# One-core recurrent trunk: small transfers on GpSimd's queue, and first slabs with two contraction tiles of four output tiles

## The chip, the cores and the metric

The kernel runs on one core of one Trainium2 chip. The metric is the device time of one execution in microseconds, lower is better, and the time of a kernel is the median of its runs.

## What is computed

One inference step of a two-layer decoder trunk (width 2048) for 288 tokens: one prompt of 256 and eight samples of 4 tokens that share the weights. Cut to what matters here:

```
layer 0:  u = x @ w_in_e                       # 2048 -> q, k, v, lru_x, z, lru_gate (6144) and 16 gate columns
          q, k, v, lru_x = causal_conv(width 4, with the last 3 rows of state_conv)
          a  = gated_delta_rule(q, k, v, g, beta, state_delta)  # 8 heads, S is 128 x 128 for each head and sample
          b  = rg_lru(lru_x, r, i, state_lru)
          mix = concat(a, b) @ w_out_e
layer 1:  u = x @ w_in_o ; mix = mlstm(q, k, v, i, f, state_c, state_n, state_m) @ w_out_o   # 8 heads
each:     x = LN(alpha*x + mix) ; x = LN(alpha*x + sqReLU-MLP(x)) ; x = x + sigmoid(x Wg) * (p Wp)
outputs:  y, and the new conv, delta, lru and mLSTM states of prompt and samples
```

All values are f32. The 16 gate columns of layer 0 give g (the decay, as a running sum along the tokens) and beta of the eight delta heads.

## The kernel before

**Matrix products.** The tokens lie along the free dimension (288 columns). An f32 product is made of three passes in a rounded format: `ah`, `bh` are the rounded values ("hi") of the activations and `al`, `bl` the rests ("lo"), `hi` and `lo` the same of the weights, and a contraction tile costs the passes hi·ah, lo·ah and hi·al, all into one PSUM tile `acc` (L416). Weights come as slabs of eight 128x128 blocks (512 KB): SyncE (SP) issues the transfer into one of four `raw` buffers (L394), ScalarE casts it to `hi` (L294), VectorE subtracts to get `lo` (L295), and TensorE spends 24 matmuls on it. `Trunk.convert` issues one slab, `top_up` keeps up to three slabs converted ahead in the mixers. An output tile (16 contraction tiles, 48 matmuls) is two slabs. There are 20,064 such matmuls, and they take the bulk of the time.

**The start.** `Trunk.load` issues on SP, in this order: x tiles 0 and 1, the first slab in two halves, x tiles 2 and 3, x tiles 4 to 7, two slabs, x tiles 8 to 15, parameters and constants. A slab holds eight contraction tiles of one output tile. The first four output tiles (`z`, `v`, `k`, `q` of head 0) are taken in groups: the lower eight contraction tiles of all four, then the upper eight, so that the fourth slab can run with x tiles 0 to 7. After three of these slabs (`GATES_AT = (3, 1)`) `gate_products` makes the 16 gate columns from a 256 KB slab `w_ab`: 32 matmuls with 32 columns of weights each, once with `ah` and once with `al`; VectorE and ScalarE then make g and beta in rows of 8 partitions, called `bl` in the trace (`delta_gates`, L701 to L727), which end with a scan (L715).

**The side work.** While TensorE runs through slabs, `tick` lets generators go one step every 12 matmuls: the eight delta heads (`delta_head`), the sample part (`delta_sample`), the eight RG-LRU blocks, and in layer 1 the mLSTM heads. Their small matmuls stand between the slabs' matmuls in TensorE's order, which is fixed when the program is built. An engine works its instructions off in order, so a small matmul whose input is late holds the slabs behind it.

**Small transfers.** SP's queue also carries, between the slabs: the convolution's state into `cin` and out of it (`sconv`, `conv`, 28 KB), `gcb` (a head's row of g from the scratch `dgc` in DRAM, broadcast to 128 partitions, 144 KB), the sample states `S` in and out (256 KB, 32 loads and 16 stores, `delta_sample`, L1010 and L1074), `wri`, `delta_p`, and in layer 1 `ngb`, `cn` in and out (514 KB) and `mc_p`. ScalarE's queue carries the gates' small transfers: `dgc`, then `dds` (g, beta, last g to DRAM) and `rs` (the same back, along the partitions); in layer 1 `dng`, `mds`, `mrs`, `dw`, `w`, `dsc`, `scB`. Pool (GpSimd) issues no transfer; it copies small pieces, for instance `ks` and `zs` (a head's sample columns, L861, L862), `gcs` (from `gcb`, L863), `v` and `k` of an mLSTM head (L1317).

**Head 0.** `dgc` and `rs` wait for the scan. From `gcb` comes the decay mask `dm`, from `rs` the factors `sw`; VectorE then makes `mq`, `X`, and the 32x32 transposes `t` (L791), and TensorE starts head 0's inversion with a small matmul that takes `t` and `cm`.

Of the kernel before, what the change touches and what calls it, by code (L numbers as in the profile page):

```python
# [37 lines left out]
C_FOLD = C_LAST + 128  # L38
C_D32 = C_FOLD + 32
# [6 lines left out]
def const_table():  # L46
# [16 lines left out]
    c[:, C_FOLD:C_FOLD + 32] = j % 32 == np.arange(32)[None]  # L63
# [79 lines left out]
def lay_out(a):  # L143
    d = {}
# [14 lines left out]
    d["w_in_e"] = pack_w(a["w_in_e"][0][:, :6144])  # L159
    d["w_ab"] = pack_gates(a["w_in_e"][0][:, 6144:])  # L160
# [46 lines left out]
GATES_AT = (3, 1)  # L207
LATE = 12

# [9 lines left out]
class Trunk:  # L219
# [73 lines left out]
    def split(self, hi, lo, src):  # L293
        self.nc.scalar.copy(hi, src)  # L294
        self.nc.vector.tensor_sub(lo, src, hi.bitcast(F32))  # L295
# [37 lines left out]
    def slabs(self):  # L333
# [9 lines left out]
        for layer in range(2):  # L343
# [11 lines left out]
            for w in group(ms[:4], gates, GATES_AT[layer]):  # L355
                yield w, False
# [22 lines left out]
    def convert(self, src, extra, parts=1):  # L379
# [4 lines left out]
        if src.shape[1] == 4:  # L384
# [3 lines left out]
            return  # L388
        lo = pools[1].tile([128, 8, 128], F32R, name="lo")
        raw = self.rawp.tile([128, 8, 128], F32, name="raw")  # L390
        n = src.shape[1]
        for k in range(0, n, n // parts):
            part = (slice(None), slice(k, k + n // parts))
            self.nc.sync.dma_start(raw[part], src[part])  # L394
            with self.behind():
                self.split(hi[part], lo[part], raw[part])
        self.ahead.append((hi, lo))
# [58 lines left out]

    def products(self, x, outer=0, between=None):
# [4 lines left out]
    def gate_products(self, x):  # L462
# [3 lines left out]
        for k in range(4):  # L466
            for i in range(2):
                for q in range(4):
                    at = 4 * q + k
                    self.nc.tensor.matmul(acc[32 * q:32 * q + 32], w[:, 32 * at:32 * at + 32], x[i](at).bitcast(F32),  # L470
                                          start=k == 0 and i == 0, stop=k == 3 and i == 1)
# [13 lines left out]
    def load(self):  # L485
        nc, t = self.nc, self.t
        self.todo = self.slabs()
        self.A = self.pair("a")
        x = self.xp.tile([128, 16, NT], F32, name="bh")
        p = self.cst.tile([128, P_END], F32, name="params")  # L490
        c = self.cst.tile([128, C_END], F32, name="consts")

        def part(k, n=4):
            nc.sync.dma_start(x[:, k:k + n], t["x"][:, k:k + n])
            self.split(*(a.tile[:, k:k + n] for a in self.A), x[:, k:k + n])
# [10 lines left out]
        nc.sync.dma_start(c, t["consts"])  # L506
# [1045 lines left out]
```

## Time and profile before

| | |
|---|---|
| median of three runs | 2912.96 us (2909.19 to 2916.35) |
| profiled execution | 2916.8 us, of which the span of instructions is 2915.0 us |
| TensorE busy | 2888.7 us, 99% of the span |
| VectorE, ScalarE, Pool busy | 1732.1, 1318.7 and 57.9 us |
| TensorE's share of the chain that ended last | 91% |
| granted TensorE clock, mean | 0.999 |

How to read it: the first part of the page has the busy time of each engine. TensorE is PE, its weight loads PEld, VectorE DVE, ScalarE ACT, GpSimd POOL, SyncE SP; a queue's own time is written with a q (SPq). A row of waits says which engine and line waited for what, in us, how many times, and the longest. A row of a timeline begins with start and duration in us, then the engine, line, operation and output<-input, and in brackets the idle time before it and what ended that.

### The profile page before, as it was taken

What the parts mean: (1) busy time and instruction counts of PE and PEld (TensorE: products, weight loads), DVE (VectorE), ACT (ScalarE), POOL (GpSimd) and SP (SyncE); (2) the same over time, 40 slices, a digit from 0 to 9 for tenths busy, and PEclk for the clock granted to TensorE, in tenths of its full rate; (3) what the DMA queues carried; (4) which work ended last, traced back from release to release, by engine and by line L of the source; (5) the groups of instructions that cost most, each with busy time, mean ns of one, the idle gap of its engine ahead of it and who ended that gap; (6) DMA issues with size and microseconds to landing.
All of it is one profiled execution on the core that took longest, in us unless ns stands there. A gap on an engine that the chain in (4) does not pass through costs nothing.

```text
span 2915.0 us, 52851 instructions
## 1 busy us (share of the span) xinstructions
PE 2888.7 (99%) x21728; PEld 2839.1 (97%) x21728; DVE 1732.1 (59%) x2872; ACT 1318.7 (45%) x2171; POOL 57.9 (2%) x197
## 2 busy tenths in 40 slices
PE   8999999999999999999999999999999999999999
PEld 7999889999999999999999999999999999999999
DVE  7787787754454454455766666567445445445574
ACT  5555676543343343443634444436334334334362
POOL 1000100000000000000000000000000000000000
PEclk9999999999999999999999999999999999999999
DMA  6444475455555555555446665554555554555543
GB/s 225 134 127 128 151 233 174 134 191 166 167 164 164 165 167 166 162 165 166 159 157 201 198 201 172 184 167 159 166 163 163 167 167 162 165 166 166 165 156 132
DMA packets 155298, 487.15 MB, mean 167 GB/s; under 512 B 28552, under 2 KB 35888, under 8 KB 155056
## 3 DMA queue, kind: packets, MB, share of 16 engines
q1 hardware_dynamic: 151632, 483.68, 51.6%
q8 instruction: 170, 2.79, 0.4%
q10 hardware_dynamic: 3424, 0.10, 0.1%
q14 instruction: 72, 0.59, 0.1%
HBM read 466.12 MB, written 17.58 MB: 166 GB/s over the span
## 4 chain that ended last, share of the span: by engine, by line
PE 91%; DVE 5%; ACT 2%; DMA 1%; issue 1%; SPq 0%; ACTq 0%; DVEq 0%
PE acc L416 86%; PE m L268 4%; DVE Y L255 1%; DVE lo L295 1%; PE m L272 1%; ACT hi L294 1%; ACT junk L265 0%; PE m L470 0%; ACT L265 0%; DMA bh<-in_x 0%; DVE cv L258 0%; DVE al L255 0%; DVE mq L258 0%; DVE bl L255 0%; DMA S<-in_sdelta 0%
## 5 line engine op out<-in xcount | busy, mean ns | idle before, releaser
L295 DVE TENSOR_TENSOR lo<-raw,hi 128x1024 fp32r<-128x1024 f32 (+1 forms) x841 | 1027.1, 1223 | 680.6 <-ACT hi L294 679.6
L294 ACT CAST hi<-raw 128x1024 fp32r<-128x1024 f32 (+1 forms) x841 | 880.1, 1048 | 1007.3 <-PE acc L416 708.4
L416 PE MATMUL acc<-ah,hi 128*128 128x288 f32 x3328 | 998.9, 301 | 6.7 <-ACT hi L294 4.9
L416 PE MATMUL acc<-bh,hi 128*128 128x288 f32 x3328 | 989.6, 298 | 0.0
L416 PE MATMUL acc<-ah,lo 128*128 128x288 f32 x3328 | 985.1, 296 | 0.2 <-DVE lo L295 0.2
L416 PE MATMUL acc<-al,hi 128*128 128x288 f32 x3328 | 982.0, 297 | 0.9 <-DVE al L295 0.5
L416 PE MATMUL acc<-bh,lo 128*128 128x288 f32 x3328 | 981.3, 295 | 0.0
L416 PE MATMUL acc<-bl,hi 128*128 128x288 f32 x3328 | 974.1, 294 | 0.6 <-DVE bl L255 0.3
L416 PEld LDWEIGHTS acc<-ah,hi 128*128 128x128 f32 x3328 | 627.1, 189 | 12.6 <-ACT hi L294 4.9
L416 PEld LDWEIGHTS acc<-bh,hi 128*128 128x128 f32 x3328 | 624.0, 188 | 7.7 <-issue 7.1
L416 PEld LDWEIGHTS acc<-ah,lo 128*128 128x128 f32 x3328 | 627.7, 189 | 3.7 <-issue 2.3
L416 PEld LDWEIGHTS acc<-al,hi 128*128 128x128 f32 x3328 | 627.3, 189 | 3.6 <-issue 1.4
L416 PEld LDWEIGHTS acc<-bl,hi 128*128 128x128 f32 x3328 | 624.9, 188 | 1.8 <-DVE bl L255 0.8
L416 PEld LDWEIGHTS acc<-bh,lo 128*128 128x128 f32 x3328 | 625.2, 188 | 0.4
L265 ACT ACTIVATE tmp<-acc 128x288 f32<-128x288 f32 x160 | 65.8, 411 | 307.8 <-PE acc L416 307.7
L255 DVE TENSOR_TENSOR tmp<-tmp 128x288 f32<-128x288 f32 x128 | 58.8, 459 | 155.0 <-ACT tmp L265 155.0
L258 DVE SCALAR_TENSOR_TENSOR Y<-Y,acc 128x288 f32<-128x288 f32 x128 | 58.2, 455 | 112.0 <-PE acc L416 112.0
L258 DVE SCALAR_TENSOR_TENSOR cv<-cin,params,cv 128x312 f32<-128x312 f32 x96 | 51.5, 536 | 0.5
L258 DVE SCALAR_TENSOR_TENSOR cn<-cn,scB,m 128x257 f32<-128x257 f32 x64 | 27.9, 478 | 18.9 <-PE m L268 18.9
L265 ACT ACTIVATE Y<-Y,params 128x288 f32<-128x288 f32 x64 | 37.5, 633 | 0.3
L294 ACT CAST bh<-tmp 128x288 fp32r<-128x288 f32 x80 | 34.7, 434 | 6.2 <-DVE tmp L258 4.4
L258 DVE SCALAR_TENSOR_TENSOR tmp<-tmp,Z 128x288 f32<-128x288 f32 x32 | 14.6, 457 | 38.3 <-ACT tmp L265 38.3
(386 smaller groups left out, 1554.0 us busy)
## 6 DMA issues: line engine op xcount, KB each, us to landing
raw<-in_w_up SPq DMA_DIRECT2D x256, 512.0 KB
raw<-in_w_down SPq DMA_DIRECT2D x256, 512.0 KB
raw<-in_w_in_o SPq DMA_DIRECT2D x96, 512.0 KB
raw<-in_w_in_e SPq DMA_DIRECT2D x95, 512.0 KB
raw<-in_w_gate SPq DMA_DIRECT2D x64, 512.0 KB
raw<-in_w_out_e SPq DMA_DIRECT2D x32, 512.0 KB
raw<-in_w_out_o SPq DMA_DIRECT2D x32, 512.0 KB
cn<-in_smlstm SPq DMA_DIRECT2D x16, 514.0 KB
```

The source lines that it names most:

```text
L255: return self.nc.vector.tensor_tensor(out=out, in0=a, in1=b, op=op)
L258: self.nc.vector.scalar_tensor_tensor(out=out, in0=a, scalar=s, in1=b, op0=op0, op1=op1)
L265: return self.nc.scalar.activation(out, a, f, **k)
L268: self.nc.tensor.matmul(out, l, r, start=start, stop=stop)
L272: self.nc.tensor.transpose(out, a, self.ident[:n, :n])
L294: self.nc.scalar.copy(hi, src)
L295: self.nc.vector.tensor_sub(lo, src, hi.bitcast(F32))
L416: self.nc.tensor.matmul(acc, l[:, k], x[r](8 * kb + k), start=at == 0, stop=at == n - 1)
```

## The change

- Nearly all small transfers go from SP's and ScalarE's queues to Pool's: `sconv`, `conv`, `rows`, `params`, `praw`, `dgc`, `dds`, `rs`, `gcb`, `S`, `delta_s`, `delta_p`, `wri`, `lru`, and in layer 1 `mm`, `dng`, `mds`, `mrs`, `dw`, `w`, `dsc`, `scB`, `ngb`, `cn`, `mc_s`, `mc_p`. They are issued in program order between Pool's copies. `S` and `wri` loads are ordered behind Pool's last `zs` copy.
- The first eight slabs come from a new weight array `w_first`: a slab holds two contraction tiles of four output tiles, so one slab needs two x tiles. x comes in finer pieces between the slabs (x tile 0 on ScalarE's queue), and each pair is split when its slab is. `Trunk.first` runs the slabs; the four products end within the last slab.
- Work that needs the parameters (`dnh`, `lru_consts`, `ea`) is ordered behind the last split of x.
- Layer 0's gates take x itself in f32, with 16 matmuls where there were 32, after five slabs (`GATES_AT = (5, 1)`).
- Seven matmuls on a constant tile (`WARM = 7`) stand at the start of TensorE's work.
- An unused block of the constants is gone (1632 to 1600 columns).

```diff
-GATES_AT = (3, 1)
+FIRST = (32, 16, 8, 0)
+GATES_AT = (5, 1)
+WARM = 7
+def pack_first(w, ms):
+    w = w[:, :6144].reshape(8, 2, 128, 48, 128)[:, :, :, list(ms)]
+    return np.ascontiguousarray(w.transpose(0, 2, 1, 3, 4).reshape(8, 128, 8, 128))
...
+    def first(self, x, between):
+        accs = [self.acc.tile([128, NT], F32, name="acc") for _ in range(4)]
+        n = [0] * 4
+        def run(m, k, p, slab, s):
+            l, r = ((slab[0], 0), (slab[0], 1), (slab[1], 0))[p]
+            self.nc.tensor.matmul(accs[m], l[:, 4 * k + m], x[r](2 * s + k), start=n[m] == 0, stop=n[m] == 47)
...
+        for s in range(8):
+            if s == between[0]:
+                between[1]()
+            slab = self.next_slab()
+            order = [(m, k, p) for k in range(2) for p in range(3) for m in range(4)]
+            if s == 7:
+                order.sort()
...
-    def gate_products(self, x):
+    def gate_products(self, parts):
...
-            for i in range(2):
+            for x in parts:
...
     def load(self):
...
+        for _ in range(WARM):
+            self.mm(warm, self.mean, self.mean)
...
-        part(0, 2)
-        self.top_up(1, 2)
-        part(2, 2)
-        part(4)
-        self.top_up(2)
+        part(nc.scalar, 0, 1)
+        nc.gpsimd.dma_start(p, t["params"])
...
+        self.convert(*next(self.todo), 2, second)
+        self.xs = pairs()
         self.top_up(3)
-        part(8)
-        part(12)
-        nc.sync.dma_start(p, t["params"])
...
-        nc.scalar.dma_start(self.dgc, gc)
+        nc.gpsimd.dma_start(self.dgc, gc)
...
-            nc.scalar.dma_start(self.rs[:, n], ds[n].rearrange("(g b) h t -> (b h t) g", g=2))
+            nc.gpsimd.dma_start(self.rs[:, n], ds[n].rearrange("(g b) h t -> (b h t) g", g=2))
...
-        nc.sync.dma_start(gcb, self.dgc[h:h + 1].to_broadcast([128, NT]))
+        nc.gpsimd.dma_start(gcb, self.dgc[h:h + 1].to_broadcast([128, NT]))
...
-            nc.sync.dma_start(s, state(h, g))
+            with self.behind([self.zlast]):
+                nc.gpsimd.dma_start(s, state(h, g))
...
-        nc.sync.dma_start(ngb, self.dng[h:h + 1].to_broadcast([128, NT]))
+        nc.gpsimd.dma_start(ngb, self.dng[h:h + 1].to_broadcast([128, NT]))
...
-            nc.sync.dma_start(cn, self.t["smlstm"][h, :, gs])
+            nc.gpsimd.dma_start(cn, self.t["smlstm"][h, :, gs])
```

SP's queue at the start of the program, before (`bh` is x here; 128x576 is two tiles of x):

```order
L494 DMA bh<-in_x 128x576
L394 DMA raw<-in_w_in_e 128x512 x2
L494 DMA bh<-in_x 128x576
L494 DMA bh<-in_x 128x1152
L394 DMA raw<-in_w_in_e 128x1024 x2
L494 DMA bh<-in_x 128x1152 x2
L505 DMA params<-in_params 128x405
L506 DMA consts<-in_consts 128x1632
L386 DMA hi<-in_w_ab 128x512
```

And after the change, where x tile 0 has gone to ScalarE's queue and the parameters to Pool's:

```order
L407 DMA raw<-in_w_first 128x512
L545 DMA bh<-in_x 128x288
L407 DMA raw<-in_w_first 128x512
L545 DMA bh<-in_x 128x576
L407 DMA raw<-in_w_first 128x1024
L545 DMA bh<-in_x 128x1152
L407 DMA raw<-in_w_first 128x1024 x2
L545 DMA bh<-in_x 128x1152
L407 DMA raw<-in_w_first 128x1024 x2
L545 DMA bh<-in_x 128x1152
L398 DMA hi<-in_w_ab 128x512
```

The second slab of eight blocks stands behind four tiles of x and half a megabyte of weights, where it stood behind eight tiles of x.

Pool's queue around head 0's scan, after the change (`bl` are the gate rows, `zs`, `ks`, `gcs` Pool's copies; before, Pool had only the copies here):

```order
L923 COPY ks<-kq 128x8x4
L1082 COPY win_149<-ks 128x4x4
L733 DMA cin_145<-in_sconv 128x56
L923 COPY ks<-kq 128x8x4
L1082 COPY win_149<-ks 128x4x4
L779 DMA dgc<-bl 8x288
L786 DMA dds<-bl 8x8x4 x2
L924 COPY zs<-z 128x8x4
L919 DMA gcb<-dgc 128x288
L737 DMA out_conv<-cin_146 128x59
L789 DMA rs<-dds 128x2x1 x2
L919 DMA gcb<-dgc 128x288
```

Head 0's `dgc`, `gcb` and `rs` now stand in one line with a copy of the next head's `z` and a store of its `v` convolution.

Pool's queue at layer 1's gates, before (`mv` and `mkq` are an mLSTM head's values and keys, `ngb` its row of the gate's maxima):

```order
L1310 COPY ksr<-mkq 128x8x4
L1311 COPY vsr<-mv 128x8x4
L1317 COPY v_17289<-mv 128x128
L1311 COPY vsr<-mv 128x8x4
L1317 COPY v_17289<-mv 128x128
L1312 COPY ngs<-ngb 128x8x4
L1326 MEMSET vt 128x2x2
```

And after:

```order
L1309 DMA dng<-ah 8x288
L1319 DMA mds<-al 8x8x4 x2
L1322 DMA mrs<-mds 128x2x1
L1324 DMA dw<-al 8x32
L1331 DMA dsc<-al 8x8
L1322 DMA mrs<-mds 128x2x1 x2
L1369 DMA ngb<-dng 128x288
L1327 DMA w_17051<-dw 32x8x1 x4
L1333 DMA scB<-dsc 128x64
L1376 COPY vsr<-mv 128x8x4
L1377 COPY ngs<-ngb 128x8x4
L1382 COPY v_17291<-mv 128x128
```

The copies of the second half of `mv`, which TensorE's transposes of `v` wait for, now stand behind fourteen transfers, of which `mrs`, `ngb`, `w` and `scB` read what others have just written to DRAM.

In TensorE's order, head 0's first matmul with `t` and `cm` stands behind 332 of the slabs' matmuls before and behind 387 after; the gates' matmuls stand behind 72 and 120, the last rows of the gates behind 96 and 144. From about 600 on the order of both kernels is the same. In VectorE's order, head 0's `z` (from the first finished product) stands ahead of most of the gates' rows in both, and all of them ahead of the scan.

## Rows read from the trace of the kernel before

**Rows 1.** Waits of PE: engine, line, for what: us, times, longest.
```profile
PE acc L416 <- ACT hi L294: 4.9, 1, 4.9
PE m L268 <- DVE t L791: 3.6, 2, 3.3
...
PE m L268 <- DVE sT L258: 1.4, 1, 1.4
...
PE m L268 <- DMA S<-in_sdelta: 1.1, 1, 1.1
```

**Rows 2.** Timeline of PE in the first 45 us.
```profile
4.95 0.61 PE L416 MATMUL acc<-ah,hi 128*128 128x288 f32 x1 [4.95 <-ACT hi L294]
...
9.05 0.61 PE L416 MATMUL acc<-ah,hi 128*128 128x288 f32 x1 [1.74 <-ACT ah L294]
...
12.36 0.61 PE L416 MATMUL acc<-al,hi 128*128 128x288 f32 x1 [0.55 <-DVE al L295]
...
18.29 0.41 PE L416 MATMUL acc<-al,hi 128*128 128x288 f32 x1
18.53 0.30 PE L416 MATMUL acc<-ah,hi 128*128 128x288 f32 x1
...
43.54 0.29 PE L416 MATMUL acc<-ah,hi 128*128 128x288 f32 x1
...
43.94 0.30 PE L416 MATMUL acc<-ah,hi 128*128 128x288 f32 x1
```

**Rows 3.** Stretches: window, length, busy per engine, PEclk, DMA share, GB/s.
```profile
5.00:10.00 5.00, 3.07 (x9) 2.11 (x9) 2.15 (x4) 1.52 (x3) 0.00 (x0) 1.00 0.95 370
10.00:15.00 5.00, 4.45 (x17) 3.97 (x18) 3.73 (x4) 4.16 (x4) 0.00 (x0) 1.00 1.04 416
...
70.00:73.00 3.00, 3.00 (x15) 3.00 (x14) 2.78 (x7) 1.71 (x3) 0.00 (x0) 0.50 0.55 145
```

**Rows 4.** Timeline of ACT in the first 22 us.
```profile
9.76 1.15 ACT L294 CAST ah<-bh 128x1152 fp32r<-128x1152 f32 x1 [0.77 <-DMA bh<-in_x]
11.05 1.05 ACT L294 CAST hi<-raw 128x1024 fp32r<-128x1024 f32 x1
```

**Rows 5.** Chain of work, 0 to 50 us: start, us, what.
```profile
23.09 4.02 PE m L470 x64
27.11 3.40 PE acc L416 x24
30.50 0.61 PE m L268 x2
```

**Rows 6.** Timeline of DVE, 33 to 49 us: head 0's `z`, and the scan.
```profile
35.63 0.38 DVE L258 SCALAR_TENSOR_TENSOR z<-silu,acc 128x288 f32<-128x288 f32 x1
...
47.45 0.74 DVE L715 TENSOR_TENSOR_SCAN bl<-bl 8x288 f32<-8x288 f32 x1
```

**Rows 7.** Chain of work, 44 to 76 us.
```profile
48.22 0.29 ACTq L717
48.55 3.36 DMA dds<-bl
51.92 4.61 DMA rs<-dds
...
67.99 0.17 DVE t L791
68.19 0.63 PE m L268 x4
```

**Rows 8.** Timeline of POOL, 26 to 75 us.
```profile
48.63 5.01 POOL L861 COPY ks<-kq 128x32 f32<-128x32 f32 x1 [3.28 <-DVE kq L258]
53.70 0.20 POOL L1019 COPY win<-ks 128x16 f32<-128x16 f32 x1
```

**Rows 9.** Issues of `out_delta_s` on SP: ns least, median, most; first and last.
```profile
L1074 SPq DMA_DIRECT2D out_delta_s<-S x16: 332/344/542, 385.0 to 426.2; - x16
```

**Rows 10.** Timeline of ACT at layer 1's gates, 1526 to 1540 us.
```profile
1533.10 2.46 ACTq L1262 DMA_DIRECT2D w<-dw  x4
1535.61 0.46 ACTq L1268 DMA_DIRECT2D scB<-dsc  x1
1536.12 0.22 ACT L265 ACTIVATE mwT<-mwT 128x16 f32<-128x16 f32 x1 [4.69 <-DMA w<-dw]
```

More of the change, by code (lines that the diff above doesn't have):

```diff
@@ L354, in slabs @@
                 ms += [("w_in_o", m) for m in range(32, 48)]
-            for w in group(ms[:4], gates, GATES_AT[layer]):
+            if layer == 0:
+                first = [t["w_first"][i] for i in range(8)]
+                first.insert(GATES_AT[0], gates)
+            else:
+                first = group(ms[:4], gates, GATES_AT[1])
+            for w in first:
                 yield w, False
@@ L388, in convert @@
             return
+        next(self.xs, None)
         lo = pools[1].tile([128, 8, 128], F32R, name="lo")
@@ L396, in convert @@
                 self.split(hi[part], lo[part], raw[part])
+            if between and k == 0:
+                between()
         self.ahead.append((hi, lo))
@@ L455, in gemms @@
                     yield accs[m]
+    def first(self, x, between):
[4 more added lines that the diff above has]
+            self.nc.tensor.matmul(accs[m], l[:, 4 * k + m], x[r](2 * s + k), start=n[m] == 0, stop=n[m] == 47)
+            n[m] += 1
+            self.count += 1
+            if self.count >= self.every:
+                self.count -= self.every
+                self.tick()
+        for s in range(8):
[5 more added lines that the diff above has]
+                order.sort()
+            for m, k, p in order:
+                run(m, k, p, slab, s)
+                if s == 7 and n[m] == 48:
+                    if m == 3:
+                        self.live -= 1
+                    yield accs[m]
+            if s < 7:
+                self.live -= 1
+        while True:
+            yield self.gemm(x)
     def products(self, x, outer=0, between=None):
@@ L619, in layer_norm, with behind @@
             low(14, 2)
-    def behind(self):
+    def behind(self, fence=None):
         ctx = ExitStack()
-        for ins in self.fence:
+        for ins in self.fence if fence is None else fence:
             ctx.enter_context(self.tc.issue_after(ins.ins))
@@ L1110, in lru_block @@
         w = lp.tile([128, 2, 128], F32, name="wri")
-        nc.sync.dma_start(w, self.t["wri"][n])
+        with self.behind([self.zlast]):
+            nc.gpsimd.dma_start(w, self.t["wri"][n])
         for _ in range(2):
@@ L1173, in gates @@
             def gates():
-                side.append(self.delta_gates(self.gate_products(x), lp, self.row_space(n_out + "l")))
+                side.append(self.delta_gates(self.gate_products([self.raw_x]), lp, self.row_space(n_out + "l")))
                 self.sides.append(side[0])
-            accs = self.products(x, between=(GATES_AT[0], gates))
+            accs = self.first(x, (GATES_AT[0], gates))
             heads, out = [], []
```

94 lines of the change are left out of this document (55 added, 39 removed).

## The prediction

> **What bounds the kernel now.** Read the waits of TensorE first. It is busy for 99% of the span, and its waits are short and few: 4.9 us before the first weights, 3.3 us for head 0's `t`, 1.4 us for `sT` in layer 1, 1.1 us for a sample state `S` [rows 1]. The span less its busy time is 26 us (2915.0 - 2888.7). So nothing done on the other engines is worth more than these gaps, plus TensorE work that is itself removed and time that a low clock costs. The second view is TensorE's timeline at the start: the first matmul at 4.95, a gap of 1.74 until 9.05 for the cast of x, one of 0.55 until 12.36, and matmuls 0.24 us apart until 18.53; later they are 0.133 us apart (43.54 to 43.94 are three steps) [rows 2]. The first is the spacing of the low clock level, 1.2 GHz, the second that of 2.4 GHz. The stretch from 70 to 73 us shows the low level again, a granted 0.50, right after the 3.3 us wait for `t` [rows 1, 3]. The DMA row says why the start has gaps: 370 and 416 GB/s from 5 to 15 us, all that it ever moves, so what lands first decides [rows 3]. The third view is the chain to head 0's `t`, the fourth the gates of layer 1.
>
> A change of 0.3%, 8.7 us, is about what a measurement of this kernel can tell from no change.
>
> **The start.** Slab 0 now needs two x tiles where it needed eight, so the order of landing fits the order of use. The first matmul comes at about 4.5 instead of 4.95 (half as much x ahead of it). Slab 0 is 24 matmuls of 0.24 us, 5.8 us, and ends at 10.3 if its second half is in time. Slab 1 stands behind 1.6 MB (four x tiles, 0.58 MB, and two slabs, 1.05 MB). Before, the cast of x tiles 4 to 7 stood behind 1.7 MB and began at 9.76 [rows 4]. The cast of a slab takes 1.05 [rows 4], so slab 1 starts at about 10.9. From there the transfers keep up: a slab and its two x tiles are 0.8 MB, about 2 us at 400 GB/s, against 3.2 us of matmuls (24 x 0.133). Seven slabs are 22.4 us, the gates take 16 matmul groups' worth instead of 32, half of 4.02, so 2.0, and the gates' rows 0.6 [rows 5]. That gives 35.9 for the 192nd matmul, where before it starts at 43.94 [rows 2]. The clock is what I am not sure of. Before, the low level lasted until 18.53, behind gaps of 1.74 and 0.55. If it lasted as long, the 7.6 us from 10.9 on would do half the work, 3.8 late: 39.7. If it rose with slab 1, 35.9. TensorE now works earlier (from 4.5, and the seven matmuls on the constant tile ahead of it) and has one short gap of 0.6 in place of those two, so I go nearer to the early end and take 36.6: 7.3 gained, 2.0 of it the gates' matmuls, bounds 4.2 to 8.0.
>
> **Head 0.** Most of that is not kept at once. `t` waits for the scan, and the scan stands on VectorE behind `z` and the gates' rows: 11.8 us from 35.63 to 47.45 [rows 6]. All four first products now end together, near the end of the last slab, so `z` can be had at 35.2 and not much earlier than before. With the same 11.8 us, and about 1.3 for the `q` convolution, whose input buffer must be read again over Pool's queue, the scan stands at about 48.3. Behind it come `dds` and `rs`, 3.36 and 4.61 [rows 7], now issued on Pool. `t` was ready at 68.2, and I expect 69.5; a Pool queue as quick as ScalarE's gives 68.5, and one Pool copy of 5.01 us instead of 0.20 in the row [rows 8] gives 73. TensorE arrives there after 195 more slab matmuls, 26.0, and 2.3 of small ones (before: 68.2 - 3.3 - 43.9 - 140 x 0.133), at 64.9. So it waits 4.6 us, more than before, and the low clock level follows as before. But it arrives with 387 slab matmuls done instead of 332. These 55 are 7.3 us of work, and `t` is 1.3 later: the net is 6.0 gained (2.5 to 7.0), and the start's size hardly matters as long as the wait is there.
>
> **Pool's issue cost.** No row shows a DMA issued by Pool. SP's and ScalarE's take 0.29 to 0.62 us [rows 7, 9, 10], Pool's copies 0.20, and 5.01 beside dense VectorE work [rows 8]. I take 0.7 each, nearer to the plain issues, with 0.3 and 1.5 as ends of a mean over many. The Trainium skill (SBUF — State Buffer, section "A bandwidth-pool intuition that's wrong (but worth ruling out)") says that a DMA from GpSimd's queue takes about 620 ns alone and about 3100 ns beside a VectorE copy that uses the port which both share. The copy of 5.01 agrees with such a hold-up; at 3100 ns for each transfer the sum below would be far over the range.
>
> **Delta's sample part.** 16 stores of `S` leave from 385.0 to 426.2, one every 2.75 us [rows 9], each with a load of the next on the same queue. On Pool that is 1.4 us of 2.75 at 0.7: it fits, and SP's slabs no longer stand between them. The wait of 1.1 for the first `S` [rows 1] could go. But a store waits for VectorE's last update, and the next load stands behind it, as does each `wri`. I take 2.5 lost, from 1.0 gained to 10 lost; at over 1.2 us per transfer the pairs alone would set the pace, and 1.5 us would cost 15 x 0.5 = 8.
>
> **Layer 1's gates.** Here the change gives and takes. ScalarE stood for 4.69 us behind `w`, and issued its four transfers in 2.46 and `scB` in 0.46 [rows 10], while the exponentials that `sT` needs came behind them. That goes, and with it up to the 1.4 us wait [rows 1]. What is late next is Pool: fourteen transfers, three of which read back what has just been written, stand ahead of the copy of `v` that TensorE transposes a microsecond before `sT`. At ScalarE's prices `scB` ends at 1536.1 and the copies at 1536.7, which is when TensorE is there: 0.7 gained. Each 0.1 us above that price adds up to 1.4. I take 1.5 lost, from 0.7 gained to 10 lost. The layer's `cn` and `conv` transfers have room: 0.5 lost. The parameters' work has VectorE's idle time to lie in: nothing.
>
> **The sum.** -6.0 + 2.5 + 1.5 + 0.5 = -1.5, and half a microsecond more for the small RG-LRU and SP back-pressure terms that I can't split: -2. The profiled run took 2916.8, so 2914.8 for it; it lies 3.8 above the median, so 2911 for the median.
>
> **Rivals.**
> - *Slower: Pool's queue sets the pace.* A transfer costs 1.2 us or more on Pool in the mean, as one in four would with 5.01 and the rest with 0.3 [rows 8]. Then layer 1's fourteen cost 11 (14 x 0.8), delta's pairs 3 to 8, head 0's net falls to 2.5 to 5, with 1.7 for clock lost after the long wait: +8 to +16, so 2921 to 2929, middle 2925. For it: VectorE is dense exactly where these transfers stand, and the one Pool instruction there took 5 us. Against it: its neighbours took 0.2. It decides from about 1.1 us per transfer. The rule of the Trainium skill named above (SBUF — State Buffer) would be this rival at a still higher price.
> - *Faster: the price is that of SP's.* `t` at 68.5 gives 7.0, layer 1's wait goes (1.4), the wait for `S` goes (1.1), and nothing else is late: -9.5, so 2903.5; 2900 if `t` also comes ahead of TensorE. For it: ScalarE and SP lose all their waits for small transfers. Against: the in-order queue with next head's items ahead of `rs`.
> - *The start doesn't do what it says.* The low clock level lasts until 18 or later, or slab 1 lands late since more transfers share the bandwidth behind it: acc 192 at 39 to 41. Since the wait for `t` swallows that, only the gates' and head 0's 55 matmuls remain, less 1 to 2: 2913.
>
> **Chances.** Forecast 0.46, the start that doesn't 0.12 (both within 0.3%), slower 0.18, faster 0.24. The range holds 2900 to 2924: it takes in the faster case and half of the slower one. Faster by over 0.3% 0.24, within 0.58, slower 0.18.
>
> **What would show it.** Right: the 192nd slab matmul at 36 to 38 us, a wait for `t` of 3.5 to 6 us with 0.50 of the clock behind it, Pool's issue rows of 0.5 to 0.9 us, small new waits at `S` and layer 1's `v`. Wrong: Pool rows of several us for a transfer; a `t` that is ready when TensorE comes; new waits of TensorE of over 3 us in 340 to 440 or 1530 to 1540; or any growth of the long middle, which the change doesn't touch beyond `praw`.

## The result, and the profile after

| | before | after |
|---|---|---|
| median | 2914.01 us (4 runs, 2909.19 to 2916.35) | 2933.55 us (4 runs, 2929.64 to 2934.01) |
| ratio of after to before, 95% interval | | 1.0066 (1.0049 to 1.0084) |
| profiled execution; its span | 2916.8; 2915.0 us | 2929.64; 2927.9 us |
| TensorE busy | 2888.7 us | 2893.7 us |
| Pool busy | 57.9 us | 178.5 us |

The changed kernel is slower by 19.5 us in the medians, and by 12.9 in the spans of the two traces: the profiled execution of before lies 2.8 above its median, that of after 3.9 below. What follows explains the 12.9 that the traces show; the 6.6 between are the spread of executions, and no trace tells where they lie. The mean granted clock gives a hint: it is 0.997 in the profiled execution of the changed kernel and 0.994 to 0.995 in its other three, so those spent more time at TensorE's low clock level.

Since TensorE's order is fixed when the program is built, the two traces are best compared by the start of the same slab matmul, counted in TensorE's timeline. This table has them for all kernels of this document (us; the last column is the span). The column 192nd has the start of the matmul that stands behind the first 192, 43.94 before [rows 2], and so on. The matmul that takes `t` stands behind 332 slab matmuls in before and queues_only, behind 404 in start_only, and behind 350 to 387 in the others: the 387th of start_only (64.4) is the only one ahead of its wait.

| kernel | median | 192nd | 387th | 1000th | 2304th | 3200th | span |
|---|---|---|---|---|---|---|---|
| before | 2914.0 | 43.9 | 79.8 | 194.9 | 450.7 | 579.4 | 2915.0 |
| after | 2933.6 | 36.2 | 76.6 | 199.9 | 460.1 | 589.1 | 2927.9 |
| start_only | 2910.6 | 36.2 | 64.4 | 190.5 | 445.8 | 574.6 | 2910.4 |
| queues_only | 2933.8 | 41.6 | 84.6 | 202.9 | 465.1 | 594.1 | 2934.6 |
| gates0_back | 2931.8 | 35.4 | 76.4 | 194.9 | 462.3 | 591.3 | 2930.3 |
| copies_behind | 2927.7 | 35.6 | 70.8 | 193.7 | 460.5 | 589.4 | 2928.7 |
| state_back | 2923.7 | 35.3 | 75.0 | 196.3 | 449.1 | 578.0 | 2919.2 |
| gates1_back | 2927.9 | 36.0 | 76.6 | 199.8 | 461.9 | 590.9 | 2927.0 |
| three_back | 2915.9 | 36.0 | 73.0 | 193.7 | 446.8 | 575.8 | 2917.4 |
| gates_early4 | 2904.7 | 36.1 | 69.0 | 185.2 | 439.0 | 567.7 | 2903.5 |
| gates_early3 | 2906.5 | 36.4 | 71.1 | 187.5 | 440.5 | 569.3 | 2905.2 |
| no_warm | 2903.8 | 35.2 | 66.0 | 182.1 | 438.8 | 567.5 | 2903.2 |

After against before: 7.8 us ahead at the 192nd, 3.2 at the 387th, 5.0 behind at the 1000th, 9.4 behind at the 2304th (the sample part of the delta heads), 9.6 at the 3200th, and 12.9 at the end (3.0 of the last 3.3 at layer 1's gates, around 1550 us). From the 192nd to the 1000th TensorE was idle for 7.6 us more than before and busy for 5.2 us more with the same slabs; in the sample part 3.2 and 1.2, at layer 1's gates 2.2 and 0.8.

TensorE's waits in the changed kernel, as [rows 1]:

```profile
PE m L275 <- DVE t L853: 8.4, 2, 8.1
PE m L279 <- POOL v L1382: 4.4, 1, 4.4
PE m L275 <- DMA S<-in_sdelta: 3.1, 2, 2.0
PE m L275 <- DVE lah L262: 2.7, 1, 2.7
```

The wait for `t` has grown from 3.3 to 8.1, that for `S` from 1.1 to 3.1, and layer 1's 1.4 for `sT` has become 4.4 for Pool's copy of `v`. `lah` is a row of the RG-LRU, whose small transfers are on Pool too.

**The start.** TensorE's timeline, as [rows 2]:

```profile
1.06 3.36 PE L275 MATMUL m<-mean 128*128 128x128 f32 x14 [1.06 <-DVE mean L536]
5.31 1.33 PE L479 MATMUL acc<-ah,hi 128*128 128x288 f32 x4 [0.89 <-ACT hi L301]
...
9.31 1.12 PE L479 MATMUL acc<-al,hi 128*128 128x288 f32 x4
10.27 0.70 PE L479 MATMUL acc<-ah,lo 128*128 128x288 f32 x4
...
23.61 2.15 PE L517 MATMUL m<-bh,hi 128*32 128x288 f32 x32
25.69 0.79 PE L479 MATMUL acc<-ah,hi 128*128 128x288 f32 x4
```

The seven matmuls on the constant tile and the sixteen of the gates stand here as two rows each. No gap is left from 5.31 to the end of the first slabs. Four matmuls take 0.96 us from start to start until 10.27 and 0.53 from there, so the high clock level comes at 10.3 instead of 18.5, and the gates take 2.1 instead of 4.0. In these first microseconds the level is read from that spacing: the granted clock of a stretch reads 1.00 there at either spacing (5 to 15 us in [rows 3]).

**Head 0.** Pool's timeline around the scan (which ends at 49.4):

```profile
45.77 2.34 POOL L923 COPY ks<-kq 128x32 f32<-128x32 f32 x1 [1.50 <-DVE kq L265]
48.17 6.99 POOL L1082 COPY win<-ks 128x16 f32<-128x16 f32 x1
55.11 0.54 POOL L733 DMA_DIRECT2D cin<-in_sconv  x1
55.64 0.22 POOL L923 COPY ks<-kq 128x32 f32<-128x32 f32 x1
55.92 0.20 POOL L1082 COPY win<-ks 128x16 f32<-128x16 f32 x1
56.16 0.53 POOL L779 DMA_DIRECT2D dgc<-bl  x1
56.70 1.20 POOL L786 DMA_DIRECT2D dds<-bl  x2
...
60.47 0.59 POOL L919 DMA_DIRECT2D gcb<-dgc  x1 [2.35 <-DMA dgc<-bl]
```

A copy of 128x16 that takes 0.2 us at 55.92 takes 6.99 at 48.17, and `dgc`, whose input is there at 49.4, is issued at 56.16. What it holds is seen in VectorE's timeline and in the chain of work:

```profile
63.76 0.43 DVE L262 TENSOR_TENSOR dm<-gcb,consts 128x256 f32<-128x256 f32 x1 [8.09 <-DMA gcb<-dgc]
```
```profile
75.39 0.24 DVE t L853
...
75.67 1.06 PE m L275 x4
```

VectorE stands for 8.09 us behind `gcb`, and `t` comes at 75.4. From the issue of `dgc` to the start of `t` it is 19.2 us; before it was 19.8 (48.22 to 67.99, [rows 7]). So the whole delay arose ahead of `dgc`: 1.2 us since the scan ends later, the rest behind the copy. Before, a Pool copy was held at the same place too (5.01, [rows 8]), but `dgc` was on ScalarE's queue.

Then the clock. Stretches of TensorE around the wait, and two later ones (window, length, busy per engine, granted clock, DMA share, GB/s):

```profile
69.00:75.00 6.00, 0.00 (x0) 0.00 (x0) 5.96 (x18) 3.52 (x10) 0.80 (x3) 0.72 0.41 144
76.00:85.00 9.00, 9.00 (x41) 9.00 (x41) 3.92 (x11) 2.98 (x8) 1.31 (x4) 0.50 0.28 84
85.50:90.00 4.50, 4.50 (x37) 4.45 (x36) 3.99 (x12) 2.49 (x12) 0.75 (x2) 1.00 0.46 141
...
413.00:416.00 3.00, 3.00 (x11) 2.30 (x10) 2.46 (x6) 2.65 (x5) 0.66 (x2) 0.50 0.63 216
...
1549.60:1553.00 3.40, 3.40 (x13) 2.94 (x11) 2.06 (x6) 2.16 (x9) 0.63 (x3) 0.51 0.21 44
```

For nine us after the wait TensorE is busy throughout at 1.2 GHz, which costs it some 4.5 us. Before, the wait of 3.3 was followed by three such us [rows 3]. The last two rows are low stretches that before did not have: one behind the wait of 2.7 for `lah`, one behind layer 1's wait of 4.4. So the new waits cost more than the idle time at all three places.

**Layer 1.** Pool's timeline at the gates:

```profile
1537.69 0.52 POOL L1309 DMA_DIRECT2D dng<-ah  x1
...
1543.77 0.74 POOL L1322 DMA_DIRECT2D mrs<-mds  x1 [1.83 <-DMA mds<-al]
1544.50 0.58 POOL L1369 DMA_DIRECT2D ngb<-dng  x1
1545.07 2.33 POOL L1327 DMA_DIRECT2D w<-dw  x4
1547.39 0.57 POOL L1333 DMA_DIRECT2D scB<-dsc  x1
...
1548.71 0.29 POOL L1382 COPY v<-mv 128x128 f32<-128x128 f32 x1
```

The copy of `v` comes 11 us after `dng`, behind fourteen transfers of 0.52 to 0.77 us and one wait for a landing. TensorE stands at its transpose from 1544.7 to 1549.05.

### The profile page after: what moved, and what is told of

Its sections match the earlier page's. It is cut to its first block, busy times and chain, and to the rows that moved or that the text cites. A ratio compares the mean times of both kernels' runs of the same rounds, so it can differ in the third digit from the quotient of the medians.

```text
span 2927.9 us, 52885 instructions
## 1 busy us (share of the span) xinstructions
PE 2893.7 (99%) x21710; PEld 2844.5 (97%) x21710; DVE 1732.4 (59%) x2876; ACT 1320.2 (45%) x2176; POOL 178.5 (6%) x410
## 4 chain that ended last, share of the span: by engine, by line
PE 90%; DVE 5%; ACT 2%; issue 1%; DMA 1%; POOL 1%; POOLq 0%; DVEq 0%; ACTq 0%
PE acc L431 84%; PE m L275 4%; DVE Y L262 1%; PE acc L479 1%; PE m L279 1%; DVE lo L302 1%; ACT hi L301 1%; DMA gcb<-dgc 0%; DMA S<-in_sdelta 0%; ACT L272 0%; POOL win L1082 0%; ACT junk L272 0%; DVE cv L265 0%; DVE bl L262 0%; PE m L517 0%
## 5 line engine op out<-in xcount | busy, mean ns | idle before, releaser
L431 PE MATMUL acc<-ah,hi 128*128 128x288 f32 x3264 | 977.2, 300 | 0.9 <-ACT hi L301 0.9
L431 PE MATMUL acc<-ah,lo 128*128 128x288 f32 x3264 | 966.2, 296 | 1.5 <-DVE lo L302 1.5
L431 PE MATMUL acc<-al,hi 128*128 128x288 f32 x3264 | 961.6, 296 | 0.3 <-DVE al L262 0.3
L431 PEld LDWEIGHTS acc<-ah,hi 128*128 128x128 f32 x3264 | 614.0, 188 | 5.8 <-issue 4.2
L431 PEld LDWEIGHTS acc<-ah,lo 128*128 128x128 f32 x3264 | 614.6, 188 | 5.1 <-issue 2.6
L431 PEld LDWEIGHTS acc<-al,hi 128*128 128x128 f32 x3264 | 614.2, 189 | 2.4 <-issue 1.2
```

What stands on the lines that cost most here:

```text
L431: self.nc.tensor.matmul(acc, l[:, k], x[r](8 * kb + k), start=at == 0, stop=at == n - 1)
```

## The experiments

In the diffs, a minus is a line of the changed kernel (or of the one named) and a plus that of the experiment. The kernel before was timed again with each group of experiments (medians of 2911.7 to 2914.2 us), and a ratio is to the median of its own group.

**1. The start alone, and the queues alone.**

start_only:
```diff
-        nc.gpsimd.dma_start(self.dgc, gc)
+        nc.scalar.dma_start(self.dgc, gc)
...
-            with self.behind([self.zlast]):
-                nc.gpsimd.dma_start(s, state(h, g))
+            nc.sync.dma_start(s, state(h, g))
```
(and likewise for every small transfer but the parameters)

> The changed kernel's start (first slabs, x in pieces, unsplit gates, seven matmuls on a constant), with every small transfer but the parameters back on the queue that it had before. Theory A (the loss comes from Pool's in-order queue, in which head 0's transfers stand behind a copy that VectorE holds up): the 192nd slab matmul at 36 us as in the changed kernel, t ready at 68 to 69.5, a wait for t of 2 to 5 us instead of 8.1, no new waits at S or at layer 1's v, and 5 to 9 us less than before in all (2905 to 2909). Rival C (the start itself is at fault, since the four first products now end together and VectorE's rows pile up): t still at 73 or later, the wait at 6 or more, and the time within 3 us of before or above it.

Measured: 2910.61 us, ratio to before 0.9991 (0.9981 to 1.0000).

```profile
PE m L275 <- DVE t L853: 4.4, 3, 3.8
PE m L275 <- issue: 2.4, 2, 1.4
PE m L275 <- DVE sT L265: 1.8, 1, 1.8
```

The waits for `S` and `v` are gone, the 192nd matmul is where it was, the wait for `t` is 3.8. But `t` is ready only at 70.4, the low level after it lasts 6.8 us, and of the 7.7 us at the 192nd matmul 4.4 are left at the 1000th. Theory A's places are right and its gain is too large: the start alone is 0 to 5 us faster than before, not 5 to 9.

queues_only (against before):
```diff
-        nc.scalar.dma_start(self.dgc, gc)
+        nc.gpsimd.dma_start(self.dgc, gc)
...
-            nc.sync.dma_start(s, state(h, g))
+            with self.behind([self.zlast]):
+                nc.gpsimd.dma_start(s, state(h, g))
```
(and likewise for every transfer that the change moves)

> The kernel before with its own start, where only the queues are changed: every small transfer that the change moves is issued by Pool, S and wri behind Pool's last zs copy. By the differences so far (the changed kernel against the run with the changed start alone: some 20 us) Theory A expects 10 to 20 us more than before: at delta's sample part 3 to 8, at layer 1's gates 3 (a wait of 4 us or more for v), and at head 0 0 to 8, less where dgc is ordered ahead of the small Pool copies, as it is here. If the queues cost little without the new start (an interaction, rival D), it is within 6 us of before.

Measured: 2933.79 us, ratio 1.0075 (1.0058 to 1.0091), as slow as the changed kernel.

```profile
PE m L268 <- DVE t L791: 9.2, 2, 8.8
...
PE m L272 <- POOL v L1319: 5.5, 1, 5.5
PE m L268 <- DMA S<-in_sdelta: 2.9, 1, 2.9
```

The same three waits. `dgc` is here ahead of the copies and issued at 45.5, 0.3 us behind the end of the scan, but a `ks` copy of 3.38 us stands ahead of `gcb`, which is issued at 50.9, and Pool's copy from it runs at 57.4. So the queues cost 20 us with the old start (2933.8 - 2914.0) and 23 with the new one (2933.6 - 2910.6): rival D, an interaction, is out.

**2. Layer 0's gate transfers back.**

```diff
-        nc.gpsimd.dma_start(self.dgc, gc)
+        nc.scalar.dma_start(self.dgc, gc)
...
-        nc.gpsimd.dma_start(gcb, self.dgc[h:h + 1].to_broadcast([128, NT]))
+        nc.sync.dma_start(gcb, self.dgc[h:h + 1].to_broadcast([128, NT]))
```
(and `rows`, `dds`, `rs` on ScalarE)

> The changed kernel with only layer 0's gate transfers (rows, dgc, dds, rs on ScalarE's queue, gcb on SP's) back where they were; all other small transfers stay on Pool. Theory A: t ready at 68 to 70 instead of 75.4, the wait for t 1 to 4 us, the low clock level behind it 3.4 us long instead of 9.7, the 1000th slab matmul at 189 to 192 instead of 199.9, and the waits at S (3.1) and layer 1's v (4.4) unchanged: 8 to 11 us less than the changed kernel, 2920 to 2925. Rival C: t at 73 or later, less than 4 us won.

Measured: 2931.77 us, ratio 1.0065 (1.0048 to 1.0082). A miss: 1.8 us won, not 8 to 11, and `t` is ready at 74.

```profile
PE acc L431 <- DVE lo L302: 4.5, 2, 3.2
PE m L275 <- DVE tg L797: 3.9, 1, 3.9
```
```profile
ACT hi L301 <- DMA dds<-bl: 5.6, 1, 5.6
```

TensorE has new waits, of 3.2 for weights and of 3.9 for `tg`. ScalarE's row tells why for `tg`: a cast of weights stands 5.6 us (until 52.1) behind an `rs` that waits for `dds` to land, and on VectorE the copy that makes `tg` (58.05) stands behind work that waits for that `rs`. The wait for weights ended earlier, at 45.4: there the subtraction that makes `lo` stood on VectorE behind the gates' rows and the convolutions. Which queue holds the chain is a matter of what stands in line: to move a waiting transfer back is not the same as to take the wait away. 5.0 us at the 1000th matmul were won, and lost again in the sample part, where TensorE now waits 3.3 and 2.4 us at the matmuls that take `wri`. Why it waits there in this trace was not followed up.

**3. The copies behind the transfers.**

```diff
-        for i, s in enumerate((kq[:, 0], kq[:, 1], v)):
-            cp(self.ks[:, i, :, :, h], self.perm(self.smp(s)))
-        self.zlast = cp(self.zs[:, :, :, h], self.perm(zsm))
+        with self.behind([self.rsl] if h < 2 else []):
+            for i, s in enumerate((kq[:, 0], kq[:, 1], v)):
+                cp(self.ks[:, i, :, :, h], self.perm(self.smp(s)))
+            self.zlast = cp(self.zs[:, :, :, h], self.perm(zsm))
```
(`rsl` is the last `rs` transfer)

> The changed kernel with all transfers on Pool, where only the small Pool copies of heads 0 and 1 (ks, zs, and win after them) are ordered behind the last rs transfer. Theory A: dgc is issued within 1 us of the end of the scan (some 49.5 to 50.5) instead of 56.2, t is ready at 69 to 70.5, the wait for t is 2 to 4 us, and 6 to 9 us are won against the changed kernel. Rival B (Pool's transfers themselves are slow: descriptors made in software, 0.54 us of issue each, beside a dense VectorE): dgc early, but gcb and rs land late all the same, t at 73 or later, and less than 4 us won.

Measured: 2927.72 us, ratio 1.0052 (1.0037 to 1.0067), 5.8 less than the changed kernel.

```profile
48.94 0.53 POOL L779 DMA_DIRECT2D dgc<-bl  x1 [2.02 <-DVE bl L777]
...
51.39 0.59 POOL L919 DMA_DIRECT2D gcb<-dgc  x1 [0.65 <-DMA dgc<-bl]
...
55.42 0.73 POOL L789 DMA_DIRECT2D rs<-dds  x1 [2.14 <-DMA dds<-bl]
56.14 0.37 POOL L924 COPY ks<-kq 128x32 f32<-128x32 f32 x2
```

All transfers are still on Pool, with the same 0.53 to 0.73 of issue. With the copies out of the way, `dgc` leaves at 48.9 instead of 56.2, `t` is ready at 69.7 instead of 75.4, the wait for it is 4.1 instead of 8.1, and the 1000th matmul comes at 193.7 instead of 199.9. That is close to theory A's numbers, and rules out B for head 0. The whole kernel is less clear: the executions of the two overlap (2924.5 to 2930.5 and 2929.6 to 2934.0), and in this trace the sample part gives all 6.2 us back (from the 1000th to the 2304th it takes 6.6 more than in the changed kernel, with waits of 2.8 for `S` and 4.0 at a matmul that takes `wri`).

**4. The sample states back.**

```diff
-            with self.behind([self.zlast]):
-                nc.gpsimd.dma_start(s, state(h, g))
+            nc.sync.dma_start(s, state(h, g))
...
-                nc.gpsimd.dma_start(self.t["delta_s"][h, :, 4 * g:4 * g + 4], s)
+                nc.sync.dma_start(self.t["delta_s"][h, :, 4 * g:4 * g + 4], s)
```
(and `wri`)

> The changed kernel with only the sample states' transfers (32 loads of S, 16 stores, and the 8 loads of wri) back on SP's queue. Theory A (a load of S waits for an earlier store of its buffer to land, and on Pool's in-order queue the next heads' small transfers and copies stand behind that wait): TensorE's waits for S (3.1 us) and for y (2.7) go, the stretch from the 1000th to the 3200th slab matmul takes 384 to 386 us as before instead of 389.2, and the wait for t (8.1) stays: 3 to 5 us less than the changed kernel. Rival B (the loss there comes from Pool's issue price on all small transfers, the RG-LRU's included): less than 2 us won.

Measured: 2923.71 us, ratio 1.0037 (1.0022 to 1.0052), 9.8 less than the changed kernel. From the 1000th to the 3200th matmul it takes 381.7 us, where the changed kernel takes 389.2 and before 384.6, and no wait for `S` or `lah` is left. In the changed kernel, the rows on the issue of `S` are (count, ns least, median, most, first and last; then the idle time before it):

```profile
L1073 POOL DMA_DIRECT2D S<-in_sdelta x32: 537/537/551, 274.3 to 428.6; - x32
...
  DMA out_delta_s<-S: 12.2, 7
```

A load waits for the store that last used its buffer, 12.2 us in seven times, and `cin`, `wri`, `out_conv` and the RG-LRU's copies stand behind it in line. On SP only the next slabs do, and three are converted ahead. The run won more than expected, since Pool's new order also issued `dgc` earlier (53.8 instead of 56.2; the wait for `t` is 5.4); layer 1's wait for `v` is 6.4 here, so the three places are not quite independent.

**5. Layer 1's gate transfers back.**

```diff
-            nc.gpsimd.dma_start(self.w4[32 * q:32 * q + 32], dw.rearrange("h b t -> (b t) h"))
+            nc.scalar.dma_start(self.w4[32 * q:32 * q + 32], dw.rearrange("h b t -> (b t) h"))
...
-        nc.gpsimd.dma_start(ngb, self.dng[h:h + 1].to_broadcast([128, NT]))
+        nc.sync.dma_start(ngb, self.dng[h:h + 1].to_broadcast([128, NT]))
```
(and `rows`, `mm`, `dng`, `mds`, `mrs`, `dw`, `dsc`, `scB`)

> The changed kernel with only layer 1's gate transfers (rows, mm, dng, mds, mrs, dw, w, dsc, scB on ScalarE's queue, ngb on SP's) back. Theory A (the copy of v stands on Pool behind them): TensorE's wait of 4.4 for v goes and the old wait of 1.4 to 1.8 for sT comes back, the low clock level after it (3.4 us long) may go, so 2.5 to 4 us less than the changed kernel; everything before 1500 us as in the changed kernel. Rival: v is late for another reason, and the wait stays at 3 us or more.

Measured: 2927.93 us, ratio 1.0053 (1.0038 to 1.0068), 5.6 less, where 2.5 to 4 were expected. The wait for `v` is gone, one of 1.43 for `sT` is back, and the stretch from the 10,200th to the 10,400th slab matmul, the only one of layer 1 that differs between before and after, takes 3.0 us less, as it took 3.0 more after the change. That is what the trace shows of the 5.6. Up to the 1000th matmul all is as in the changed kernel; the sample part takes 1.9 us more in this trace.

**6. All three.** The copies ordered as in 3, with the queues of 4 and 5.

> The changed kernel with the three repairs together: head 0's and head 1's small Pool copies behind the last rs, the sample states' transfers and wri back on SP, layer 1's gate transfers back on ScalarE and ngb on SP. Head 0's transfers, the convolutions', cn and the rest stay on Pool. If the loss is the sum of the three places (one by one they won 5.8, 9.8 and 5.6 us), it is 15 to 21 us faster than the changed kernel, 2912 to 2918, and near the run with the changed start alone (2910.6): t ready at about 70, no waits for S, 1.4 to 1.8 for sT instead of 4.4 for v. If a part of the loss comes from the mere load of Pool's queue, it stays above 2920.

Measured: 2915.94 us, ratio to before 1.0008 (0.9998 to 1.0018), 17.6 less than the changed kernel. The three places are 17.6 of the 22.9 us between the medians of the changed kernel and start_only (10.5 of 17.5 in the spans of the traces). One by one they won 5.8, 9.8 and 5.6, in sum 21.2; by the ratios to before it is 4.1, 8.4 and 3.8 one by one and 16.9 together, each give or take 6 or 7 us by the intervals. So the sum holds within the noise, and a single one of the three is hardly clear of it: what ties each to its place is the trace. What the rest comes from was not tested; this trace still has `t` at 72, and a wait of 2.5 for `vt` of a later mLSTM head, which a Pool instruction makes.

**7. What holds a Pool copy.** Probes behind the end of the kernel before. Their core:

```diff
+            two = lambda i: self.tt(o[i % 4], a, b, ALU.subtract)
+            one = lambda i: self.ts(o[i % 4], a, 3.0, ALU.mult)
+            mix = lambda i: self.tt(o[i % 4][:, 0:256], ps[:, 0:256], b[:, 0:256], ALU.subtract)
...
+                for i in range(count):
+                    op(i)
...
+                    nc.gpsimd.tensor_copy(last, go)
```

> The kernel before, with a probe behind its end that computes nothing of the output: six stretches of VectorE instructions back to back (twice 8 subtractions of two f32 tiles in SBUF, twice 14 multiplications of one f32 tile in SBUF by a constant, twice 24 subtractions of an SBUF tile from PSUM), and in each, from its first instruction on, either one Pool copy of 128x32 or one Pool transfer of the same tile to DRAM and one back. Theory A: beside the two-input subtractions the copy takes as long as they do (8 to 10 us), beside the PSUM ones 0.2 to 0.5; the one-input stretch is open. The transfer is issued in 0.5 to 0.6 us in all three and lands 2 to 4 us later. Rival B: the transfer beside the two-input stretch is issued or lands 3 us or more later than beside the PSUM one.

> The kernel before with a second probe behind its end, which again computes nothing of the output: as the first, but VectorE's instructions write four tiles in turn, so that one can begin before the one ahead has ended, as the slabs' and the convolutions' do. Stretches: 8 two-input subtractions beside a Pool copy, the same beside a Pool transfer to DRAM and back, 14 one-input multiplications beside a copy, 24 subtractions from PSUM beside a copy, and 6 two-input ones in turn with 6 from PSUM beside a copy. In the first probe, where each instruction waited for the one ahead, the copy got through at the end of one instruction (1.09 us). Theory A2 (a Pool copy gets the port only in a gap between VectorE's instructions): 8 us or more beside the two-input stretch, 0.2 beside the PSUM one, several us in the mixed one. Rival: 1.1 to 1.3 us again, so that what held the copy for 7 us at 48 us is something else (the small gate rows, or the copy's own inputs). The transfer is issued in 0.5 to 0.7 us either way.

> The kernel before with a third probe behind its end, which computes nothing of the output. In the second, a Pool copy was held for 8.4 us by one-input multiplications back to back, for 1.2 by two-input ones. Here VectorE's stretches have the forms of the stretch that held the copy in the kernel, each beside a strided Pool copy like ks (and a plain one after it): two-input subtractions of 128x1024; the convolution's form with a per-partition factor, 128x312; the gate rows' form, 8x288; the two last in turn, beside a plain copy and beside a strided one; a mix of all with a one-input row; and one-input rows of 8x288. If only one-input instructions hold, the copy takes under 1.5 us in the first five and several in the last. If the strided copy needs many gaps, it is slow (2 us and more) in the first five and the plain one is not. If the per-partition factor or the short rows hold, it is slow there alone.

Pool's timeline of the second probe: beside two-input subtractions a copy and then two transfers; beside one-input multiplications a copy; beside subtractions from PSUM; beside two-input ones and PSUM ones in turn.

```profile
2905.79 1.18 POOL L1536 COPY plast<-pgo 128x32 f32<-128x32 f32 x1 [1084.87 <-DVE pgo L1531]
2915.25 0.68 POOL L1539 DMA_DIRECT2D pdram<-pgo  x1 [8.28 <-DVE pgo L1531]
2917.37 0.55 POOL L1540 DMA_DIRECT2D plast<-pdram  x1 [1.45 <-DMA pdram<-pgo]
2924.18 8.43 POOL L1536 COPY plast<-pgo 128x32 f32<-128x32 f32 x1 [6.25 <-DVE pgo L1531]
2932.88 0.21 POOL L1536 COPY plast<-pgo 128x32 f32<-128x32 f32 x1 [0.28 <-DVE pgo L1531]
2941.26 1.14 POOL L1536 COPY plast<-pgo 128x32 f32<-128x32 f32 x1 [8.16 <-DVE pgo L1531]
```

The transfers are not held: the load that waits for the store to land is issued 2.1 us after it, and in the first probe 2.0 to 2.1 beside all three kinds. That speaks against slow transfers (rival B) beside these kinds; beside one-input multiplications that overlap, the stretch that held the copy longest, no transfer was tried. The copy is held for one instruction of the two-input kind (1.18; a subtraction takes 1.21), and for a whole stretch of fourteen one-input multiplications of 128x1024 (8.43). So A2 failed: it expected 8 us or more beside the two-input kind. The third probe, with the forms of the kernel: 0.32 to 0.46 beside the convolution's or the gate rows' form, 0.77 to 0.89 beside both in turn, whether the copy was strided or not, 0.21 to 0.23 beside one-input rows of 8x288, and beside the mix:

```profile
2956.04 1.15 POOL L1539 COPY plast<-pgo 128x32 f32<-128x32 f32 x1 [6.86 <-DVE pgo L1534]
2957.25 2.11 POOL L1542 COPY plast<-pgo 128x32 f32<-128x32 f32 x1
```

So a short copy beside a dense VectorE takes from 0.2 to over 8 us, by what VectorE runs, and 2.1 is the most that a mix like the kernel's gave. The 6.99 at 48 us were not reproduced; what in that stretch adds up to them stays open. The traces of the kernels narrow it down: twelve Pool copies in them take over 2.2 us, all between 43 and 56 us. VectorE works through each of the twelve without a pause, and each ends 0.06 to 0.09 us behind the end of a VectorE instruction; in the kernel before, the copy of 5.01 ends at 53.64 and VectorE first pauses at 53.56. That the copy ahead of `dgc` delayed it is shown by run 3 without that.

**8. From the start alone to a faster kernel.** In start_only the gates' rows end late (the scan begins at 47.8). The gates can run a slab earlier if x and the constants are issued a little earlier. Against start_only:

```diff
-GATES_AT = (5, 1)
+GATES_AT = (4, 1)
...
-            for k, at in ((2, 2), (4, 4), (6, None), (8, 8), (10, None), (12, 12), (14, None)):
+            for k, at in ((2, 2), (4, 4), (6, None), (8, 8), (10, 12), (12, None), (14, None)):
...
-                if k == 14:
+                if k == 12:
```

> The run with the changed start alone (small transfers back on their old queues), with layer 0's gates one slab earlier (after four slabs), the last four x tiles and the constants issued a little earlier for it. Of the two things that t waits for, z and the gates' rows, this moves the rows: the scan ends at 44 to 47 instead of 48.5, t is ready at 66 to 69 instead of 70.5, and the small matmul that takes it stands behind 368 slab matmuls instead of 387 (2.5 us earlier). Theory A expects 0 to 4 us less than the start alone, 2906 to 2911. If VectorE's order around z is what holds t (rival C), t stays at 70 and the kernel is 0 to 3 us slower than the start alone.

Measured: 2904.69 us, ratio to before 0.9975 (0.9965 to 0.9984), 5.9 less than start_only and a little more than the 0 to 4 expected.

```profile
PE m L275 <- DVE sT L265: 1.7, 1, 1.7
PE m L275 <- DVE cv L265: 1.7, 1, 1.7
PE m L275 <- DVE t L853: 1.4, 2, 1.0
```

`t` is there at 63.8, earlier than expected, the wait for it is 1.0, and the low level does not come back:

```profile
72.00:78.50 6.50, 6.50 (x52) 6.39 (x51) 4.95 (x19) 4.10 (x16) 1.55 (x3) 1.00 0.63 204
```

In start_only the same 6.5 us had 30 matmuls at a granted 0.50. This version is faster than the changed kernel, and by 0.25% than the one before. Two variants:

> As the run with the gates after four slabs, but after three, with all x tiles from 8 on issued before them. The gates' rows start 3 us earlier still, t is behind 350 slab matmuls instead of 368. What t waits for then is the second k/q convolution and VectorE's rows, not the gates: t at 63 to 66 while TensorE is there at 60 to 62, so a wait of 2 to 4 us: 1 to 4 us slower than with the gates after four. If the earlier x costs the slabs nothing and t follows, up to 2 us faster.

Measured: 2906.48 us (ratio 0.9978, 0.9968 to 0.9987). The wait for `t` is 0.7, but a new one of 1.7 for the scan appears at 46 us; no gain over four slabs.

no_warm:
```diff
-WARM = 7
+WARM = 0
```

> The fastest run so far (changed start, old queues, gates after four slabs) without the seven matmuls on the constant tile at TensorE's start. If they matter to the clock, the 192nd slab matmul comes 0.5 to 3 us later than 36.1 and the low clock level lasts longer than 9.8 us; if they do nothing, both stay and the time is within 1 us.

Measured: 2903.80 us (ratio 0.9972, 0.9962 to 0.9983). Without the seven matmuls the matmuls are 0.13 apart from 8.0 us on and the 192nd comes at 35.2, where the run with them has 9.8 and 36.1. But one trace does not settle what the seven do to the clock, since with the same start and the seven in place the rise itself varies. In three of nine traces (gates0_back, copies_behind, state_back) the slabs' matmuls are 0.13 apart from the first on; this row of copies_behind has four of them in 0.69, as the changed kernel has from 10.27 on:

```profile
5.92 0.69 PE L479 MATMUL acc<-al,hi 128*128 128x288 f32 x4
```

In the other six the high level begins between 9.7 and 10.7 us. The 192nd matmul hardly follows: it comes at 35.3 to 35.6 in the three and at 36.0 to 36.4 in the six. In the time of the whole kernel the seven bring nothing that these runs show.

## Why the prediction was wrong

The forecast was 2911 and the range ended at 2924; measured was 2933.6.

- **The start: right.** 36.2 for the 192nd matmul, forecast 36.6. The first matmul came at 5.31, not 4.5, and the clock rose at 10.3, near the early end. The place of the rise is partly luck: with this start it lay between 5.3 and 10.7 us in nine traces, and the 192nd matmul between 35.3 and 36.4.
- **Head 0: this step failed.** The scan was forecast at 48.3 and stood at 48.6. `t` was forecast at 69.5 and came at 75.4, outside its own range (73). The trace of before had the row that mattered, a Pool copy of 5.01 [rows 8], and Pool's new order showed the same copies directly ahead of `dgc`. I took the 5.01 for a far end instead of asking whether it would happen again at the same place, beside the same VectorE work. It did, with 6.99, and the copy that nobody waited for before was now ahead of the chain that TensorE waits for. With that copy out of the way (run 3) `t` came at 69.7, close to the forecast.
- **The clock after the wait: mis-sized.** I let it follow "as before", some 1.7 us. After a wait of 8.1 there were nine us at half speed, some 4.5. The forecast net of 6.0 gained became 5.0 lost at the 1000th matmul, 11.0 worse: 6 of it is `t` (75.4, not 69.5), some 3 the longer low stretch, and 2 are not located. No term stood for low stretches elsewhere, and two came, behind the new waits in the sample part and in layer 1.
- **Pool's price: right.** Forecast 0.7 a transfer, measured 0.52 to 0.77 in all rows of the changed kernel. So the rival "Pool's queue sets the pace" had the better time (2921 to 2929, still short of 2933.6) with the wrong mechanism: not the price, but what stands in line ahead. The rule named there, of the Trainium skill (SBUF — State Buffer, section "A bandwidth-pool intuition that's wrong (but worth ruling out)"), gives a transfer from GpSimd's queue about 3100 ns beside a VectorE copy. No run here shows such a hold-up of a transfer: its issue took 0.68 and its landing some 2 us beside two-input work. It was Pool's copies that were held (8.43 beside one-input f32 work in SBUF).
- **Delta's sample part: mis-sized.** 4.4 lost (the stretch from the 1000th to the 2304th), forecast 2.5 in a range to 10. The mechanism named, a load behind a store that must land, is the one that run 4 shows. One sum there is off by its own rows: a pair of transfers fills the 2.75 us only at 1.4 us each, and at 1.5 the loss is 15 x 0.25, some 4, not 8. And the half microsecond gained that the sum puts down for the RG-LRU and SP has no row; a wait of 2.7 for the RG-LRU's `lah` came instead.
- **Layer 1: mis-sized.** 3.0 lost, forecast 1.5: a wait of 4.4 for `v` in place of 1.4 for `sT`, less a wait of 0.7 behind it that went, and 0.8 of longer busy time with the low stretch. That `v` would be next was right.
- **The rest.** The long middle didn't change. The sum by the trace is 5.0 + 4.4 + 0.2 + 3.3 = 12.9; it is above the 2 gained of the forecast by 14.9, of which 11.0 at head 0.

## What to carry to other kernels

A queue with in-order work is not free because its engine is idle 98% of the time: before something is moved to it, list what will stand ahead of it at each place, take the longest duration that each of those ever had in the trace, and ask whether it will be long again there. A row that costs nothing because nobody waits for it becomes a price as soon as a chain is put behind it. And where TensorE's low clock level follows a wait, the wait is to be costed with a stretch at half speed: here TensorE worked some 3, 7 and 9 us at half speed behind the waits of 3.3, 3.8 and 8.1 for `t`, but only some 3 behind layer 1's 4.4, so take a range.

## What was not expected of the hardware

- A Pool copy of 128x32 took 0.21 us beside VectorE work that reads PSUM, 1.2 beside two-input subtractions in SBUF, and 8.43, the whole stretch, beside one-input multiplications of 128x1024 in SBUF; with instructions that waited for each other it took 1.1 and 0.6.
- Pool's transfers were issued in 0.52 to 0.77 us in the changed kernel, whatever VectorE did beside them. In the other traces two stores of `S` stand out, with 0.95 (copies_behind) and 1.63 (gates1_back).
- With one and the same start the high clock level began with the first slab matmul (5.3 to 5.5 us) in three traces and at 9.7 to 10.7 in six; without the seven matmuls on a constant tile it began at 8.0 in the one trace taken.
